# TensorE in written order in two MLPs, and block 2's norm work spread over more weight tiles

## The chip, the cores and the metric

The kernel runs on one core of one Trainium2 chip. The metric is device time of one execution in microseconds, the median of several runs. The engines are named as in the profile: PE is TensorE (PEld its weight loads), DVE is VectorE, ACT is ScalarE, POOL is GpSimd, SP is the engine whose queue issues the DMAs.

## The reference, cut to what matters

Two transformer blocks on 512 tokens of width 1024, in fp32. The change touches the MLP at the end of each.

```python
# block 1: D_FF = 4096
x = x + jnp.square(jax.nn.relu(rmsnorm(x, norm_ffn) @ ffn_w1)) @ ffn_w2
...
# block 2: D_FF_2 = 2816
u = rmsnorm_2(x, norm_ffn_w[l])
up, gate = jnp.split(u @ w_ffn_up[l], 2, axis=-1)
a = causal_dwconv_2(up, ffn_conv_w[l], ffn_conv_b[l])     # 3 taps along the tokens
x = x + (jax.nn.silu(a) * gate) @ w_ffn_down[l]
return rmsnorm_2(x, norm_final_w)
```

## The kernel before

**Tiling.** Activations are held transposed, features on the 128 partitions and 512 tokens along the row, so x is eight tiles of 128 x 512. A weight *tile* is 128 x 128; a *column* is the eight tiles that make one output tile of 128 x 512. Weights come in units of eight tiles (`wts`, 512 KB) through four `raw` buffers. Each unit, and each activation, is split into a high part (ScalarE, `S.copy` to fp32r) and a low part (VectorE, `V.tensor_sub`), five buffers `whi` and `wlo`; `mm3` (L466 to L468) multiplies with three matmuls, high x high, high x low, low x high. A plain column is 24 matmuls of 512 columns into one of four "mm" PSUM banks.

**Pairs.** Most hidden columns of both MLPs go two at a time through `pairg` (L351): seven products of 12 matmuls of 256 columns each, 84 in all, where the two plain columns would take 48 of 512, the length of 96. The products are, in order, B11, V1, B21, V7, B22, V6, T4. On the weight side they need sums of weights, each split in six steps (`seven_steps`; `sraw` the sums, `a`, `s75`, `s64`, `b` the operands). On the activation side they need differences made by `rights` (L397), three steps for each of four pairs of x tiles: s0 two ScalarE scalings, s1 five short VectorE operations (L416 to L421), s2 two splits (L534, L535). A pair fills four banks; the first is freed early by a copy `c0` (L385, ScalarE), the others by four VectorE additions (L391 to L394) into `q`. In block 1 pairs take "mm" and "sm" banks in turn; in block 2 all take the four "sm" banks. There the hidden numbers 3, 4, 6, 7, 9, 10, 12, 13, 15, 16, 18, 19 (each an up and a gate column) are pairs, the others plain.

**What is written where.** The program is emitted as straight code. `defer(n, fn)` emits `fn` once `n` more weight tiles have been taken; `wst["i"]` counts them. Tile 0 of an MLP is its first weight tile. SP's queue follows the written order (`manual_schedule` around the whole build). The order on all other engines is planned when the program is compiled: instructions are taken by a model of the machine, an earlier written one first among those that the model holds for ready, so an engine may run ahead of the written order where the model sees it wait.

**Block 1's MLP** (L1312 on): two plain and two paired hidden steps, then four groups; each takes eight down columns (`ffn_w2`) over the eight hidden tiles of its group, with the next group's pairs between them. In the last group nothing stands between its last pair (hidden 15) and its eight down columns. `rb2`, made of the sums of squares (`wide_later`, two matmuls with a matrix of ones, L621 and L622), is used when down columns are added to x; it is emitted at tile 44 (`WIDE1`).

**Block 2's MLP** (L1674 on): the input sums `acc` are split and summed by L621 and L622, the rstd row `rb` follows by a chain of VectorE operations (L628, L551 to L566, one more emitted per tile). A plain hidden (`hidden2`) is an up and a gate column, `zp` = up x `rb` (L1713), which frees the up bank, the convolution (L1590 on ScalarE, two L1592 on VectorE), silu (L1715), a product with the gate bank (L1716), a split. In a pair the same is done from `q` (`hidden7`, L1686 to L1698). Three groups, 0 to 7, 8 to 15, 16 to 21; behind each the eight down columns, with the first hidden of the next group ahead of them. The last group's down columns are done for one half of the tokens and then the other; each half ends with the sums for the final norm, one ones-matmul over seven tiles (L1794) and one over the last (L1796), fp32.

**Queues around the change.** `rb` starts at tile 3, `rights` at 5 + `VD` x pair (`VD` = 4), so at tiles 5 to 19. `zp` of hidden 0 is emitted after its two columns, at tile 16, of hidden 1 at 32, of hidden 2 at 48, where the first pair (hidden 3) begins.

Of the kernel before, what the change touches and what calls it, by code (L numbers as in the profile page):

```python
# [52 lines left out]
VD = 4  # L53
# [111 lines left out]
def build(tc, A, out, stage=99):  # L165
    nc = tc.nc
    ctx = ExitStack()
    with ctx:

        ctx.enter_context(tc.manual_schedule(engines={mybir.EngineType.SP}))  # L170
        _build(ctx, tc, nc, A, out, stage)


def _build(ctx, tc, nc, A, out, stage):
# [8 lines left out]
    def nm(s):  # L183
        cnt[0] += 1
        return f"{s}_{cnt[0]}"
# [7 lines left out]
    def tmp(shape=(P, T)):  # L193
        return ap_.tile(list(shape), F32, tag="t2", bufs=NSLOT, name=nm("tmp"))
# [4 lines left out]
    def tinyc(n):  # L199
        return ap_.tile([P, n], F32, tag=nm("tinyc"), bufs=1, name=nm("tinyc"))  # L200

    def bank(kind="mm"):
        return pp.tile([P, T], F32, tag=kind, bufs=4, name=nm(kind))
# [234 lines left out]
    def defer(n, fn):  # L438

        late.append((wst["i"] + n, fn))  # L440
        late.sort(key=lambda e: e[0])
# [84 lines left out]
    def split(src, g=None, shape=(P, T)):  # L526

        hi, lo = t2(F32R, shape), t2(F32R, shape)
        split_to(hi, lo, src, g)
        return hi, lo  # L530
# [16 lines left out]
    def rsqrt_g(r, a, lat=0.3):  # L547

        t, h = (tiny(a.shape[-1]), tiny(a.shape[-1])) if a.shape[-1] < 64 else (tmp(a.shape), tmp(a.shape))
        al = 0.375 ** 0.5  # L550
        V.tensor_scalar(r.bitcast(I32), a.bitcast(I32), -0.5, float(0x5F3759DF),  # L551
                        op0=ALU.mult, op1=ALU.add)
        yield 0.0, lat
        V.tensor_mul(t, r, r)
        yield 0.0, lat
        V.scalar_tensor_tensor(out=h, in0=t, scalar=al, in1=a, op0=ALU.mult, op1=ALU.mult)
        yield 0.0, lat
        V.scalar_tensor_tensor(out=t, in0=h, scalar=-1.25 / al, in1=h, op0=ALU.add, op1=ALU.mult)
        yield 0.0, lat
        V.scalar_tensor_tensor(out=r, in0=t, scalar=1.875, in1=r, op0=ALU.add, op1=ALU.mult)  # L560
        yield 0.0, lat
        V.tensor_mul(t, r, r)
        yield 0.0, lat
        V.scalar_tensor_tensor(out=t, in0=t, scalar=-0.5, in1=a, op0=ALU.mult, op1=ALU.mult)
        yield 0.0, lat
        V.scalar_tensor_tensor(out=r, in0=t, scalar=1.5, in1=r, op0=ALU.add, op1=ALU.mult)  # L566
# [22 lines left out]
    def row_bc(c, nt, dst=None):  # L589

        ps = bank("sm")
        for i in range(nt):
            PE.matmul(ps[:, i * P:(i + 1) * P], lhsT=c[:, i:i + 1].to_broadcast([P, P]),
                      rhs=ident, start=True, stop=True)
        r = dst if dst is not None else ap_.tile([P, T], F32, tag="t2", bufs=NSLOT, name=nm("rbc"))
        S.copy(r[:, :nt * P], ps[:, :nt * P])
        return r
# [18 lines left out]
    def wide_later(acc, eps, rbt, at, square):  # L616

        def part():
            hi, lo = split(acc)
            ps = bank("sm")  # L620
            PE.matmul(ps, lhsT=ones_r, rhs=hi, start=True, stop=False)  # L621
            PE.matmul(ps, lhsT=ones_r, rhs=lo, start=False, stop=True)  # L622
            if square:
                V.tensor_scalar(rbt, ps, 1.0 / D, eps, op0=ALU.mult, op1=ALU.add)
                V.reciprocal(rbt, rbt)
                return
            a = tmp()
            V.tensor_scalar(a, ps, 1.0 / D, eps, op0=ALU.mult, op1=ALU.add)  # L628
            step(rsqrt_g(rbt, a))

        def step(g):
            if next(g, None) is not None:
                defer(1, lambda: step(g))

        defer(at, part)

    def acc_tile():
        return ap_.tile([P, T], F32, tag="t2", bufs=NSLOT, name=nm("acc"))
# [7 lines left out]
    acc = acc_tile()  # L646
# [11 lines left out]
    rb = row_bc(rc, 4)  # L658
# [553 lines left out]
    acc = acc_tile()  # L1212
# [87 lines left out]
    acc = acc_tile()  # L1300
# [8 lines left out]
    xs = xs2  # L1309


    rb2 = acc_tile()  # L1312
    wide_later(acc, 1e-6, rb2, WIDE1, True)
    rops, steps = rights(x, "norm_ffn", xs)
# [68 lines left out]
    acc = acc_tile()  # L1383
# [4 lines left out]
    for what, n, g in ffn_order():  # L1388
# [15 lines left out]
        if n == 7:  # L1404
            for k in range(8 * g, 8 * g + 8):
                hs.pop(k)
    xs = xs2

    rc12, rc, rb, rb1 = tinyc(8), tinyc(4), acc_tile(), acc_tile()

# [251 lines left out]
    acc = acc_tile()  # L1662
# [8 lines left out]
    xs = xs2  # L1671


    rb = acc_tile()  # L1674
    wide_later(acc, 1e-5, rb, 3, False)

    rops2, steps = rights(x, "norm_ffn_w_2", xs)
    for j, f in enumerate(steps):
        defer(5 + VD * (j // 3) + j % 3, f)

    def hidden7(i):
        hl = (t2(F32R), t2(F32R))
# [77 lines left out]
    for hf in range(2):  # L1760
        ts = slice(hf * H, (hf + 1) * H)
        acc = acc_tile()
# [143 lines left out]
```

## Time and profile before

| what | value |
|---|---|
| median of 3 runs | 1552.65 us (1549.92 to 1555.24) |
| the profiled execution's own time | 1555.27 us |
| its span in the trace | 1553.5 us |
| block 1's MLP in it | about 413 to 765 us |
| block 2's MLP in it | about 1161 us to the end |
| TensorE busy | 97% of the span |
| VectorE busy | 70% of the span |

The trace is of one execution, so terms worked out from it belong to 1555.27 us. TensorE's matmuls are pipelined: the bars of neighbours overlap, and the step from one start to the next is what a matmul costs in a run of them. The granted clock of a stretch (PEclk) is a share of TensorE's full speed.

### The profile page before, as it was taken

How to read it: one execution, taken by the hardware profiler on the slowest of the kernel's cores; microseconds unless marked ns; L12 is line 12 of the kernel's file. 1: busy time of each engine (PE TensorE's matmuls, PEld its weight loads, DVE VectorE, ACT ScalarE, POOL GpSimd, SP SyncE). 2: the span in 40 equal slices, each digit the busy share in tenths (PEclk: the TensorE clock that was granted, in tenths of full speed). 3: DMA queues.
4: the chain of work that ended last, by engine and by line, in shares of the span. 5: the costliest groups of instructions: out<-in, count | busy, mean ns of one | idle time of the engine just before them, and what ended most of it. 6: DMA issues, size and time to landing. Idle time of an engine off the chain costs nothing.

```text
span 1553.5 us, 21399 instructions
## 1 busy us (share of the span) xinstructions
PE 1512.2 (97%) x8336; PEld 1292.5 (83%) x8336; DVE 1080.4 (70%) x1759; ACT 705.8 (45%) x1169; POOL 147.9 (10%) x162
## 2 busy tenths in 40 slices
PE   8999999999999999999999999999998899999996
PEld 6887898888888888888888888888887888988886
DVE  6887685554786787766688677245547877887667
ACT  6665555443564353535354344333334442443343
POOL 0002110200201211011400000000020002002101
PEclk9999999999999999999999999999999999999999
DMA  6033335221222233223043222222221232224221
GB/s 252 22 108 99 114 133 190 96 68 55 82 91 87 95 108 103 95 97 122 23 161 122 82 75 81 83 93 91 97 93 43 93 122 80 84 82 136 77 74 55
DMA packets 51509, 149.94 MB, mean 97 GB/s; under 512 B 9552, under 2 KB 14032, under 8 KB 51408
## 3 DMA queue, kind: packets, MB, share of 16 engines
q1 hardware_dynamic: 51264, 148.32, 28.5%
q8 instruction: 65, 1.06, 0.3%
q14 instruction: 36, 0.29, 0.1%
q10 hardware_dynamic: 144, 0.26, 0.1%
HBM read 143.97 MB, written 3.28 MB: 95 GB/s over the span
## 4 chain that ended last, share of the span: by engine, by line
PE 88%; DVE 6%; ACT 3%; issue 1%; DMA 1%; SPq 0%; POOL 0%; DVEq 0%; ACTq 0%; POOLq 0%
PE mm L466 23%; PE mm L468 23%; PE mm L467 23%; PE sm L468 4%; PE sm L466 4%; PE sm L467 4%; DMA raw<-wts 1%; ACT whi L263 1%; DVE wlo L315 1%; DVE wlo L265 1%; ACT whi L310 1%; ACT t L1095 0%; DVE wlo L267 0%; PE sm L586 0%; DVE t L1807 0%
## 5 line engine op out<-in xcount | busy, mean ns | idle before, releaser
L466 PE MATMUL mm<-t,whi 128*128 128x512 f32 (+1 forms) x1696 | 646.6, 381 | 10.3 <-ACT whi L259 6.7
L468 PE MATMUL mm<-t,wlo 128*128 128x512 f32 (+1 forms) x1696 | 643.2, 380 | 1.9 <-DVE wlo L267 1.4
L467 PE MATMUL mm<-t,whi 128*128 128x512 f32 (+1 forms) x1696 | 642.9, 379 | 0.2 <-DVE t L535 0.2
L466 PEld LDWEIGHTS mm<-t,whi 128*128 128x128 f32 x1696 | 320.2, 189 | 71.2 <-ACT whi L259 6.7
L468 PEld LDWEIGHTS mm<-t,wlo 128*128 128x128 f32 x1696 | 320.2, 189 | 67.3 <-DVE wlo L267 2.7
L467 PEld LDWEIGHTS mm<-t,whi 128*128 128x128 f32 x1696 | 320.3, 189 | 61.5 <-DVE t L538 0.5
L263 ACT CAST whi<-raw 128x1024 fp32r<-128x1024 f32 x202 | 211.3, 1051 | 303.3 <-PE mm L467 138.6
L265 DVE TENSOR_TENSOR wlo<-raw,whi 128x1024 fp32r<-128x1024 f32 x189 | 236.5, 1252 | 78.1 <-ACT whi L263 77.7
L466 PE MATMUL sm<-t,whi 128*128 128x256 f32 (+1 forms) x464 | 132.0, 285 | 4.2 <-ACT t L534 2.3
L467 PE MATMUL sm<-t,whi 128*128 128x256 f32 (+1 forms) x464 | 131.7, 284 | 0.5 <-DVE t L535 0.5
L468 PE MATMUL sm<-t,wlo 128*128 128x256 f32 (+1 forms) x464 | 131.7, 284 | 0.0
L580 POOL TENSOR_TENSOR acc<-acc,tmp 128x512 f32<-128x512 f32 (+1 forms) x37 | 52.8, 1432 | 467.7 <-ACT tmp L576 463.9
L315 DVE TENSOR_TENSOR wlo<-sraw,whi 128x1024 fp32r<-128x1024 f32 x52 | 72.9, 1404 | 34.6 <-ACT whi L310 34.2
L310 ACT CAST whi<-sraw 128x1024 fp32r<-128x1024 f32 x52 | 54.5, 1048 | 88.0 <-PE mm L467 69.3
L466 PEld LDWEIGHTS sm<-t,whi 128*128 128x128 f32 x464 | 88.1, 190 | 5.9 <-ACT t L534 2.5
L467 PEld LDWEIGHTS sm<-t,whi 128*128 128x128 f32 x464 | 88.2, 190 | 1.6 <-DVE t L535 0.7
L468 PEld LDWEIGHTS sm<-t,wlo 128*128 128x128 f32 x464 | 88.2, 190 | 0.4
L1441 DVE TENSOR_TENSOR tmp<-mm,acc 128x512 f32<-128x512 f32 x46 | 31.7, 689 | 48.9 <-PE mm L468 46.9
L1398 POOL TENSOR_TENSOR res<-res,tmp 128x512 f32<-128x512 f32 x24 | 38.9, 1636 | 250.0 <-DVE tmp L1396 236.0
L310 ACT CAST whi<-raw 128x1024 fp32r<-128x1024 f32 x26 | 27.3, 1050 | 67.7 <-PE mm L467 37.0
L466 PE MATMUL sm<-t,t 128*128 128x256 f32 (+1 forms) x156 | 47.0, 302 | 7.3 <-ACT t L310 7.0
L302 DVE TENSOR_TENSOR sraw<-raw,raw 128x1024 f32<-128x1024 f32 x26 | 33.0, 1269 | 25.3 <-DMA raw<-wts 25.2
(384 smaller groups left out, 1971.9 us busy)
## 6 DMA issues: line engine op xcount, KB each, us to landing
raw<-wts SPq DMA_DIRECT2D x259, 512.0 KB, 3.3
res<-xT SPq DMA_DIRECT2D x16, 256.0 KB, 5.5
yT<-t SPq DMA_DIRECT2D x6, 256.0 KB, 2.2
tmp<-tmp SPq DMA_DIRECT2D x20, 64.0 KB, 2.0
gm<-gm SPq DMA_DIRECT2D x4, 256.0 KB, 4.5
dn<-ch SPq DMA_DIRECT2D x4, 256.0 KB, 2.3
tmp<-memT SPq DMA_DIRECT2D x4, 256.0 KB, 2.7
cst<-const SPq DMA_DIRECT2D x1, 576.0 KB, 6.9
```

The costliest lines, as they stand in the source:

```text
L263: S.copy(hi, r)
L265: defer(LO, lambda r=r, hi=hi, lo=lo: V.tensor_sub(lo, r, hi.bitcast(F32)))
L302: V.tensor_tensor(t["s75"].rearrange("p (a b) -> p a b", a=2), r3, r1[:, T:].unsqueeze(1).to_broadcast([P, 2, T]), op=ALU.add)
L310: S.copy(t[n][0], s)
L315: V.tensor_sub(t[n][1], src(), t[n][0].bitcast(F32))
L466: PE.matmul(ps, lhsT=ahi, rhs=bhi, start=start, stop=False)
L467: PE.matmul(ps, lhsT=ahi, rhs=blo, start=False, stop=False)
L468: PE.matmul(ps, lhsT=alo, rhs=bhi, start=False, stop=stop)
L580: eng.tensor_add(acc[:, :w], acc[:, :w], dst[:, :w])
L1398: G.tensor_add(x[n], x[n], t)
L1441: V.tensor_mul(t, ps, rb)
```

## The change

All TensorE instructions of block 1's MLP, and all from block 2's MLP to the end of the kernel, are put in a region in which TensorE issues in the written order. The other engines' order, and which of their instructions stands beside which, is planned as before, around that. In block 2's MLP the input sums and the rstd row start at tile 8 in place of 3, and the three steps of each pair of `rights` at 10, 18, 26 and 34 in place of 5, 9, 13 and 17.

```diff
+    mlp = ExitStack()
+    mlp.enter_context(tc.manual_schedule(engines={mybir.EngineType.PE}))
     rb2 = acc_tile()
     wide_later(acc, 1e-6, rb2, WIDE1, True)
     rops, steps = rights(x, "norm_ffn", xs)
...
             for k in range(8 * g, 8 * g + 8):
                 hs.pop(k)
     xs = xs2
+    mlp.close()
...
+    ctx.enter_context(tc.manual_schedule(engines={mybir.EngineType.PE}))
     rb = acc_tile()
-    wide_later(acc, 1e-5, rb, 3, False)
+    wide_later(acc, 1e-5, rb, 8, False)
 
     rops2, steps = rights(x, "norm_ffn_w_2", xs)
     for j, f in enumerate(steps):
-        defer(5 + VD * (j // 3) + j % 3, f)
+        defer(10 + 8 * (j // 3) + j % 3, f)
```

## Rows read from the trace of the kernel before

**Rows 1.** Page, part 1: busy us, share of the span, instructions of an engine

```profile
PE 1512.2 (97%) x8336; PEld 1292.5 (83%) x8336; DVE 1080.4 (70%) x1759; ACT 705.8 (45%) x1169; POOL 147.9 (10%) x162
```

**Rows 2.** By stretch: length, busy PE, PEld, DVE, ACT, POOL (instructions), PEclk, DMA, GB/s

```profile
468.30:474.50 6.20, 4.37 (x15) 3.40 (x14) 6.17 (x9) 2.46 (x5) 0.00 (x0) 0.72 0.38 137
...
726.00:764.80 38.80, 38.80 (x169) 31.38 (x168) 25.89 (x33) 21.39 (x31) 19.49 (x21) 1.00 0.13 41
1161.40:1184.00 22.60, 22.60 (x99) 18.31 (x98) 21.15 (x34) 10.75 (x15) 0.20 (x2) 1.00 0.20 70
1184.00:1198.20 14.20, 9.55 (x38) 7.55 (x37) 9.53 (x16) 6.98 (x10) 0.20 (x2) 0.76 0.00 0
...
1207.50:1218.60 11.10, 6.29 (x30) 5.99 (x30) 8.02 (x12) 5.16 (x9) 0.10 (x1) 0.69 0.14 48
1218.60:1265.00 46.40, 45.94 (x333) 42.95 (x332) 39.85 (x53) 22.15 (x30) 0.30 (x3) 1.00 0.33 107
...
1386.00:1393.00 7.00, 4.51 (x25) 4.00 (x24) 5.23 (x7) 3.27 (x6) 0.10 (x1) 0.76 0.22 75
...
1161.40:1265.00 103.60, 93.68 (x541) 82.61 (x540) 84.08 (x123) 50.15 (x68) 0.81 (x8) 0.93 0.22 73
...
1467.00:1482.00 15.00, 15.00 (x129) 15.00 (x129) 9.83 (x12) 6.60 (x8) 0.00 (x0) 1.00 0.37 116
```

**Rows 3.** Timeline, TensorE, head of block 2's MLP; [idle before <-releaser]

```profile
1188.70 0.39 PE L466 MATMUL sm<-t,whi 128*128 128x256 f32 x1 [2.34 <-ACT t L534]
...
1191.90 0.80 PE L466 MATMUL mm<-t,whi 128*128 128x512 f32 x1 [1.81 <-DVE zp L1713]
...
1212.64 0.58 PE L466 MATMUL sm<-t,t 128*128 128x256 f32 x1 [4.81 <-ACT t L310]
```

**Rows 4.** Timeline, VectorE, the same head

```profile
1166.89 0.69 DVE L535 TENSOR_TENSOR t<-acc,t 128x512 fp32r<-128x512 f32 x1
...
1177.10 0.68 DVE L566 SCALAR_TENSOR_TENSOR acc<-tmp,acc 128x512 f32<-128x512 f32 x1
...
1186.43 0.42 DVE L416 TENSOR_TENSOR t<-t,t 128x256 f32<-128x256 f32 x1
...
1191.16 0.68 DVE L1713 TENSOR_TENSOR zp<-mm,acc 128x512 f32<-128x512 f32 x1
```

**Rows 5.** Timeline, three engines, end of block 1's MLP

```profile
716.52 0.39 PE L466 MATMUL mm<-t,whi 128*128 128x512 f32 x1
...
722.61 1.14 ACT L1363 CAST t<-q 128x512 fp32r<-128x512 f32 x2
...
723.26 1.29 DVE L1368 TENSOR_TENSOR t<-q,t 128x512 fp32r<-128x512 f32 x2 [2.96 <-ACT t L1363]
```

**Rows 6.** Timeline, TensorE, between the two token halves at the end

```profile
1521.81 0.28 PE L466 MATMUL mm<-t,whi 128*128 128x256 f32 x1
...
1524.19 0.70 PE L1794 MATMUL sm<-acc,cst 128*128 128x256 f32 x2
...
1525.09 0.65 PE L1796 MATMUL sm<-acc,cst 128*128 128x256 f32 x2
```

**Rows 7.** Timeline, three engines, from hidden 6 to hidden 7

```profile
1252.24 0.40 PE L466 MATMUL mm<-t,whi 128*128 128x512 f32 x1
...
1253.32 0.50 PE L468 MATMUL mm<-t,wlo 128*128 128x512 f32 x1 [0.46 <-DVE wlo L267]
...
1253.37 0.36 ACT L385 COPY t<-sm 128x256 f32<-128x256 f32 x1
...
1255.52 0.69 DVE L391 TENSOR_TENSOR q<-sm,t 128x512 f32<-128x512 f32 x1
```

**Rows 8.** Timeline, TensorE, first pair of block 1's MLP

```profile
442.08 0.38 PE L466 MATMUL mm<-t,t 128*128 128x256 f32 x1 [1.54 <-ACT t L310]
...
443.47 0.33 PE L468 MATMUL mm<-t,t 128*128 128x256 f32 x1
```

**Rows 9.** Timeline, TensorE, first down column of block 1's MLP

```profile
470.55 0.38 PE L466 MATMUL sm<-t,whi 128*128 128x256 f32 x1 [1.83 <-ACT whi L310]
```

## The prediction, made before the change was run

> **What bounds the kernel now.** I read the share of busy time first: TensorE is busy 97% of the span [rows 1]. So only two things can move the time: places where TensorE waits, and places where its granted clock is low. The second view cuts the span into stretches and counts matmuls in each [rows 2]. Its two undisturbed rows give the price of one step. In 726.0 to 764.8 us 168 steps of 512 columns take 38.8 us, 0.231 us each; in 1467 to 1482 some 127 steps of 256 columns (129 with those that its edges cut) take 15.0 us, 0.118 us each. With these two numbers any stretch can be priced, and what is over is lost.
>
> In 1184.0 to 1198.2 there are 38 matmuls, 21 of 256 and 17 of 512 columns: 2.5 + 3.9 = 6.4 us of work in 14.2, 7.8 us lost. In 1207.5 to 1218.6 there are 30 of 256 columns, 3.5 us of work in 11.1: 7.6 lost. Both are at the head of block 2's MLP, together 15.4 us. In 468.3 to 474.5, near the head of block 1's MLP, 4 short and 9 long steps (2.6 us) leave 3.6 lost, and in 1386 to 1393 25 short steps leave 4.1 lost [rows 2]. The granted clock in these four rows is 0.69 to 0.76, so each loss is a wait and then some steps at the lower of the two clock levels, 1.2 GHz instead of 2.4.
>
> The timeline of the head of block 2's MLP says why. TensorE had taken 21 matmuls of the first paired columns (hidden 3) ahead of the last plain ones (hidden 2), and waited 2.34 us for a split of `rights`; then 1.81 us for the first `zp` (L1713), which frees the PSUM bank that up column 2 wants; then 4.81 us for the fourth weight operand of the pair [rows 3]. On VectorE the rstd row `rb` ends at 1177.8 (L566), but L1713 starts only at 1191.16, with the five subtractions and splits of three pairs of `rights` in front of it (the third at 1186.43) [rows 4]. `rights` was emitted at tiles 5 to 19, `zp` of hidden 0 at tile 16.
>
> **The change, part by part.** No instruction is added or removed; orders change. The moved steps issue work on ScalarE, VectorE and (two matmuls) TensorE, no DMA and nothing on POOL, and SP's order stays as written.
>
> *Spread of rb and rights (block 2).* The sums start at tile 8 instead of 3, `rights` at 10, 18, 26, 34 instead of 5, 9, 13, 17. Now only the first pair of `rights` is written ahead of `zp` of hidden 0, so `zp` can follow `rb` at about 1177.8. Up column 2 wants its bank when the four columns before it are done, at about 1184 where the first pair's matmuls begin [rows 2], and hidden 3, after two more columns of 5.55 us, starts near 1195; the last `rights`, written at tile 36, has until then. Both waits of [rows 3] would be covered. The floor is VectorE: it did 84.1 us of work in the 103.6 us from 1161.4 to 1265.0. At the 86% that it reached in 1218.6 to 1265.0 that takes 97.8 us, a gain of 5.8; at the 94% of 1161.4 to 1184.0 it takes 89.4, a gain of 14.2 [rows 2]; all of the loss is 15.4. I take 92%, near the upper row because there, as here, its queue was never empty: 91.4 us, a gain of 12.2. The two ones-matmuls on the input sums now stand at tile 8, one column of 5.55 us behind the stage's begin at 1161.4, so at 1167.0. The low half of the sums is there at 1167.58 [rows 4]: TensorE waits up to 0.6; I count 0.4.
>
> *Written order, end of block 1's MLP.* The last group of eight down columns comes right behind its last pair, whose 84 matmuls end at 716.5. The squares of that pair are split on ScalarE from 722.61 (two of 0.57) and on VectorE from 723.26 to 724.55 [rows 5]. TensorE now fills this with tiles of later columns. In written order it does six tiles of the first (18 x 0.231 = 4.2 us, to 720.7), waits for the seventh and is through with the eighth at 725.1. By then it has done 24 matmuls; before, in the same 8.6 us without a gap, 37. Cost 13 x 0.231 = 3.0 us; queued behind are the other seven columns, and block 2 behind these. Behind a wait of 1.83 us [rows 9] the clock was low and cost 1.8 more (3.6 lost less 1.83). Bounds 3.0 to 4.8; I take 3.9.
>
> *Written order, end of block 2's MLP.* Each half of the tokens ends with the sums for the final norm, L1794 and L1796. TensorE now runs 24 matmuls of the second half before and between them, from 1521.81 on; the sums start at 1524.19 and the last ends near 1525.7 [rows 6]. In written order those 24 come behind: 24 x 0.118 = 2.8 us, and up to 1.8 of low clock. Bounds 2.8 to 4.6; I take 3.7. Queued behind L1794 are then all columns of the second half, and the tail waits for them.
>
> *Written order, pair behind pair.* The second pair of a plain-pair-pair cycle needs a "sm" bank that the copy `c0` (L385) frees. At 1252.2 the copy is late (1253.37 on ScalarE), and the next bank comes with L391 at 1255.52 on VectorE; TensorE fills with nine 512-column matmuls and loses 0.46 us of wait, 0.7 in all [rows 7]. In written order it waits to 1253.8 and again from 1255.3 to 1256.2: 2.6 instead of 0.7, 1.9 worse. The pattern stands three times (1253, 1361, 1397): 5.7. Below, it can be nothing, as the place of the copy in ScalarE's queue is planned anew. I take half, 2.9. For this repeating gap the Trainium skill (Perfetto Trace Analysis, section Optimization Strategy of Identifying Performance Opportunities) says that the same gap repeating on the engine that should be saturated can mean too little SBUF or PSUM for the next tile. The rows agree so far that a bank copy stands beside each gap; by that rule a new order would not help and the whole 5.7 would be paid, 2.8 us more than my sum.
>
> *Written order, third product of a pair.* Four times, first at 442.08, the low half of operand `b` is later than the high half, and matmuls of the fourth product fill in (TensorE takes it up at 443.47 [rows 8]). In written order that wait shows: 1.0 us there, 0.4 to 0.5 at 461, 1246 and 1353, 2.4 in all; nothing if `b` is planned earlier. I take 2.0.
>
> *The two other losses* (468, 1386) wait for ScalarE's queue (L310), which the change does not touch by itself. They could vanish (7.7 with the clock) or grow by what TensorE no longer fills (some 3). I count a gain of 1.5.
>
> **The sum.** Gain 12.2 + 1.5 = 13.7; cost 0.4 + 3.9 + 3.7 + 2.9 + 2.0 = 12.9. Net 0.8 us shorter. The profiled execution took 1555.27 us (a span of 1553.5), 2.6 above the median of 1552.65, so I put the new median at 1551.9: the head of block 2's MLP is won, and the places that TensorE had filled out of order give it back. Three runs of before lie 5.3 us apart; about 0.3%, 4.7 us, is what a measurement can tell from no change.
>
> The Trainium skill (Perfetto Trace Analysis, Matmul Optimizations) warns that TensorE's power follows its use, so that matmuls should run back to back. The trace shows it: clock 0.72 around a wait of 1.83 us [rows 2, 9]. It speaks against the two end pieces; at full price for both the sum would be 1.8 us longer.
>
> **Rivals.** *The new waits get covered (faster).* VectorE's and ScalarE's orders are planned around TensorE's; with a fixed TensorE, copies and splits may come on time. Then only the data waits of the two ends stay (3.0 + 2.8 + 0.4 = 6.2), against 14.4 of the 15.4 and 3.5 of the 7.7: 11.7 shorter, 1541. For it: at the head VectorE's order, not its work, is the cause [rows 4]. Against: at the two ends the chain of data itself is late [rows 5, 6].
>
> *VectorE stays the floor (slower).* Behind the head come pairs 3, 4, 6, 7, where VectorE is 86% busy. If it does no better than that, the gain is 5.8, and every new wait is paid in full: 4.8 + 4.6 + 5.7 + 2.4 + 0.4 = 17.9. That is 12.1 longer, 1564.8. It decides once the head's gain falls under the written order's price; at full price that is for any gain up to 15.4, at mine below 12.9 less the 1.5. For it: the 86%. Against: that stretch also did weight splits for later columns.
>
> *The change does little of what it says.* Where nothing waits, as in 726 to 764.8, TensorE already follows the written order; and the plan for VectorE might keep `zp` behind `rights`. Then 1552.65.
>
> **How the numbers follow.** Chances: forecast 0.44 (1545 to 1559), covered waits 0.28 (1541), VectorE's floor 0.22 (1564.8), little 0.06. The forecast's own range is its bounds: gain 5.8 to 15.4, ends 5.8 to 9.4, pairs 0 to 5.7. Of it 0.08 lies under 1548.0, 0.07 above 1557.3. Faster: 0.28 + 0.08 = 0.36; same 0.29 + 0.06 = 0.35; slower 0.22 + 0.07 = 0.29. The range goes from 1538, a little below the covered waits, to 1565, the floor itself, and leaves out some 0.2.
>
> **What the profile of after would show.** Right: `zp` of hidden 0 within 2 us behind L566; no matmul of 256 columns before the sixth plain column; the stretch from up column 0 to the end of hidden 7 some 12 us shorter; a TensorE wait of about 2.5 us in the first of block 1's last eight down columns, and one of about 2.3 at the first L1794, neither there before. Wrong: `zp` still behind the second and third `rights`; no wait at those two ends; or waits of 2 us and more inside hidden 3 to 7 in place of the old ones, which would be VectorE's floor.

## The result and the profile after

| | us, median (lowest to highest) | against the kernel before (95% interval) |
|---|---|---|
| before | 1551.66 (1549.92 to 1555.24) | 1 |
| after | 1570.32 (1566.77 to 1570.69) | 1.0112 (1.0088 to 1.0136) |
| predicted | 1551.9 (1538 to 1565) | |

The change makes the kernel 1.1% slower. The time lies above the range, and above the 1564.8 of the rival "VectorE stays the floor". The profiled execution of after took 1570.69 us with a span of 1568.9, 15.4 more than the span of before. (The profiled execution of before was one of its longer ones, so the medians lie 18.7 apart, the spans 15.4.)

Page of after, the head and part 1, columns as in [rows 1]:

```profile
span 1568.9 us, 21401 instructions
...
PE 1515.6 (97%) x8336; PEld 1294.9 (83%) x8336; DVE 1081.1 (69%) x1759; ACT 706.0 (45%) x1169; POOL 147.3 (9%) x162
```

The instruction counts are those of before [rows 1], and the busy times lie within 3.4 us of them: nothing was added. The share of busy time shows nothing of a change of order. The 3.4 us more on TensorE go with a slightly lower granted clock, 0.989 over the span where before had 0.991. So the 15 us are waits, and steps at the lower clock behind them.

Stretches of after, columns as in [rows 2]: the first pair of block 1, the end of its MLP, the head of block 2's MLP, hidden 6, two places where a pair stands behind a pair, the pair whose matmuls lost 4.1 us near 1386 in before (they now run some 10 us later), and the sums between the token halves:

```profile
436.50:446.00 9.50, 6.78 (x40) 6.16 (x39) 7.32 (x11) 6.22 (x13) 0.00 (x0) 0.82 0.33 109
721.00:729.00 8.00, 5.37 (x17) 3.72 (x16) 3.02 (x6) 4.39 (x6) 0.00 (x0) 0.79 0.28 87
1203.00:1220.20 17.20, 8.07 (x38) 7.01 (x37) 12.02 (x20) 7.06 (x12) 0.20 (x2) 0.60 0.09 30
1247.50:1254.50 7.00, 5.52 (x31) 5.10 (x31) 4.16 (x7) 1.86 (x3) 0.10 (x1) 0.76 0.23 77
1258.00:1264.00 6.00, 3.73 (x29) 3.35 (x29) 5.34 (x8) 2.78 (x5) 0.00 (x0) 1.00 0.43 124
1369.00:1376.50 7.50, 4.69 (x36) 4.14 (x35) 7.13 (x10) 2.56 (x5) 0.00 (x0) 1.00 0.59 192
1394.00:1401.00 7.00, 6.25 (x52) 6.00 (x51) 5.17 (x7) 3.40 (x6) 0.10 (x1) 1.00 0.21 75
1529.00:1541.00 12.00, 9.75 (x63) 8.97 (x62) 8.48 (x22) 4.38 (x11) 0.00 (x0) 0.86 0.01 2
...
1167.10:1212.50 45.40, 36.99 (x168) 29.82 (x166) 38.07 (x61) 22.78 (x32) 0.31 (x3) 0.93 0.13 47
```

They are read with the step prices of the prediction. In 1203.0 to 1220.2, 38 short steps are 4.5 us of work, so 12.7 of 17.2 are lost. In 1394 to 1401, 52 short steps are 6.1 of 7.0 us, so of the old loss near 1386 about 1 us is left. The last row is for VectorE: from the first up column of block 2's MLP to the end of the long wait it was busy 38.07 of 45.4 us, 84%.

Timeline of after, TensorE, the rows with the waits (idle time and its releaser in brackets):

```profile
440.23 0.39 PE L466 MATMUL mm<-t,t 128*128 128x256 f32 x1 [1.81 <-ACT t L310]
441.47 0.57 PE L468 MATMUL mm<-t,t 128*128 128x256 f32 x1 [0.73 <-DVE t L315]
...
724.37 0.50 PE L466 MATMUL mm<-t,whi 128*128 128x512 f32 x1 [2.41 <-ACT t L1366]
...
1213.12 0.58 PE L466 MATMUL sm<-t,whi 128*128 128x256 f32 x1 [8.22 <-ACT t L534]
...
1260.32 0.39 PE L466 MATMUL sm<-t,whi 128*128 128x256 f32 x1 [1.38 <-ACT t L385]
1262.88 0.35 PE L466 MATMUL sm<-t,whi 128*128 128x256 f32 x1 [0.89 <-DVE q L391]
...
1398.12 0.39 PE L468 MATMUL sm<-t,t 128*128 128x256 f32 x1 [0.75 <-DVE t L315]
...
1535.34 0.70 PE L1799 MATMUL sm<-acc,cst 128*128 128x256 f32 x2 [2.11 <-DVE acc L580]
```

Where [rows 3] had three long waits at the head, there is one of 8.22 us, for the last pair of `rights`. Most other rows are places where before showed no such wait, since TensorE took something else meanwhile [rows 5 to 7]; at the first pair of block 1 one of 1.54 us has become 1.81 and 0.73 [rows 8], and at 1398 a short wait for the low half of `b` is what is left of the old one.

The same head on VectorE and ScalarE, timeline of after:

```profile
1183.85 0.69 DVE L566 SCALAR_TENSOR_TENSOR acc<-tmp,acc 128x512 f32<-128x512 f32 x1
1184.58 0.69 DVE L1718 TENSOR_TENSOR zp<-mm,acc 128x512 f32<-128x512 f32 x1
...
1202.52 1.23 DVE L315 TENSOR_TENSOR wlo<-sraw,whi 128x1024 fp32r<-128x1024 f32 x1
1203.66 1.29 DVE L535 TENSOR_TENSOR t<-t,t 128x512 fp32r<-128x512 f32 x2
1204.86 0.68 DVE L1718 TENSOR_TENSOR zp<-mm,acc 128x512 f32<-128x512 f32 x1
...
1205.64 0.72 ACT L1594 ACTIVATE tmp<-zp,colt 128x512 f32<-128x512 f32 x1 [2.12 <-DVE zp L1718]
1207.97 0.72 ACT L1720 ACTIVATE tmp<-tmp,colt 128x512 f32<-128x512 f32 x1 [1.61 <-DVE tmp L1596]
1209.45 0.62 ACT L534 CAST t<-tmp 128x512 fp32r<-128x512 f32 x1 [0.75 <-DVE tmp L1721]
1209.97 0.72 ACT L410 ACTIVATE t<-res,colt 128x512 f32<-128x512 f32 x1
```

The first `zp` follows `rb` at once, as wanted (in [rows 4] it started 13 us behind the end of it). But the `zp` of hidden 1 comes only at 1204.86, behind a weight split and the splits of `rights`, and the scalings for the last `rights` (L410) stand in ScalarE's queue behind that hidden's chain, at 1209.97.

To account for the whole, I take for each matmul the time to the start of the next one, less its step price, and add up what is over (us):

| place | before | after | change | predicted |
|---|---|---|---|---|
| head of block 2's MLP, to hidden 4 | 16.0 | 13.5 | -2.6 | -12.2 and +0.4 |
| operand `b` of hidden 6 (1248) | 0 | 3.6 | +3.6 | in the row of third products |
| end of block 1's MLP (721) | 0 | 4.6 | +4.6 | +3.9 |
| sums between token halves (1530) | 0.7 | 5.0 | +4.2 | +3.7 |
| pair behind pair (1259, 1369, 1405) | 2.2 | 9.1 | +6.9 | +2.9 |
| third products (438, 463, 1361) | 2.6 | 6.8 | +4.2 | +2.0 |
| the two others (468, and 1386, in after 1397) | 8.0 | 3.4 | -4.6 | -1.5 |
| sum | | | +16.3 | -0.8 |

Over the whole trace it is +15.5; of the -0.8 left over, 0.5 lies ahead of block 1's MLP, the rest is spread over small differences. The short fp32 steps of the sums between the halves are priced like the others, so 0.7 to 0.8 us of that row stands there without any wait.

### The profile page after: what moved, and what is told of

It reads as the page before. It is cut to its first block, busy times and chain, and to the rows that moved or that the text cites. A ratio compares the mean times of both kernels' runs of the same rounds, so it can differ in the third digit from the quotient of the medians.

```text
span 1568.9 us, 21401 instructions
## 1 busy us (share of the span) xinstructions
PE 1515.6 (97%) x8336; PEld 1294.9 (83%) x8336; DVE 1081.1 (69%) x1759; ACT 706.0 (45%) x1169; POOL 147.3 (9%) x162
## 4 chain that ended last, share of the span: by engine, by line
PE 85%; DVE 8%; ACT 4%; issue 2%; DMA 1%; SPq 0%; POOL 0%; DVEq 0%; ACTq 0%; POOLq 0%
PE mm L466 23%; PE mm L468 23%; PE mm L467 23%; PE sm L468 4%; PE sm L466 4%; PE sm L467 4%; DVE wlo L265 1%; ACT whi L263 1%; DVE wlo L315 1%; DMA raw<-wts 1%; ACT whi L310 1%; DVE t L535 1%; DVE t L315 0%; DVE q L391 0%; DVE tmp L1596 0%
## 5 line engine op out<-in xcount | busy, mean ns | idle before, releaser
L310 ACT CAST whi<-sraw 128x1024 fp32r<-128x1024 f32 x52 | 54.6, 1050 | 93.9 <-PE mm L467 65.2
L310 ACT CAST whi<-raw 128x1024 fp32r<-128x1024 f32 x26 | 27.3, 1052 | 59.3 <-PE mm L467 32.8
L302 DVE TENSOR_TENSOR sraw<-raw,raw 128x1024 f32<-128x1024 f32 x26 | 32.7, 1259 | 26.3 <-DMA raw<-wts 26.2
```

What stands on the lines that cost most here:

```text
L302: V.tensor_tensor(t["s75"].rearrange("p (a b) -> p a b", a=2), r3, r1[:, T:].unsqueeze(1).to_broadcast([P, 2, T]), op=ALU.add)
L310: S.copy(t[n][0], s)
```

## Experiments

Two theories on the written order: A, each matmul that the planner took out of order covered a wait that now shows; against it, that the order costs by what it does to other queues. On the head of block 2's MLP: F, VectorE's work up to the first pair is the floor; O, the planned order of VectorE's and ScalarE's queues makes the wait; B, the spread itself costs. "The head lost" below means the sum of the first two rows of the table: 16.0 before, 17.0 after.

### One part alone

Written order in block 1's MLP only (of the change, only this is kept):

```diff
+    mlp = ExitStack()
+    mlp.enter_context(tc.manual_schedule(engines={mybir.EngineType.PE}))
...
+    mlp.close()
```

> The kernel before with TensorE in written order in block 1's MLP alone. Theory A (each matmul that the planner had taken out of order covered a wait, and the wait now shows): the waits at 438 to 445 and at 721 to 728 of the trace of the changed kernel come back, block 1's MLP is 6 to 7 us longer, block 2 is as before; 1558 us. Rival B (the written order itself costs little, the loss is made where the norm work was spread in block 2): within 2 us of the kernel before.

Measured 1561.22 us, ratio 1.0064 (1.0049 to 1.0079). Its places lost what they lose in after: 5.1 at 438, 0.7 at 463, 4.7 at 722; block 2's head stayed at 15.2. The median rose by more than the 7 us that theory A expected; the trace itself is 5.7 us longer than the one of before.

Written order from block 2's MLP on, with the tiles of before:

```diff
+    ctx.enter_context(tc.manual_schedule(engines={mybir.EngineType.PE}))
     rb = acc_tile()
     wide_later(acc, 1e-5, rb, 3, False)
```

> The kernel before with TensorE in written order from block 2's MLP on, the norm work at its old tiles. Theory A: the ones-matmuls at tile 3 wait some 4 us for the input sums, up column 2 waits some 7 us for the late eviction of up column 0, then no matmul of hidden 3 waits as long as 4.8 us; pair behind pair, third products and the sums between the token halves cost 8 to 10 us as in the changed kernel; 1558 to 1566 us, so the spread was worth some 2 to 5 us of it. Rival B: the spread is what costs, so this is within 3 us of the kernel before.

Measured 1559.69 us, ratio 1.0051 (1.0036 to 1.0066); the trace is of the shortest execution, 1556.83. The pairs lost 2.8, 3.6 and 2.8 us, the third products 1.0 each, as in after. The head lost 13.2, in other places: 5.4 at the ones-matmuls, which at tile 3 come before the sums are there (TensorE's timeline), and 5.8 at operand `b`. The wait of some 7 us that was expected at up column 2 did not come.

```profile
1163.49 0.49 PE L621 MATMUL sm<-t,ones_r 128*128 128x512 f32 x1 [2.67 <-ACT t L534]
...
1204.84 0.38 PE L466 MATMUL sm<-t,t 128*128 128x256 f32 x1 [3.60 <-ACT t L310]
```

The spread alone, TensorE planned freely:

```diff
-    wide_later(acc, 1e-5, rb, 3, False)
+    wide_later(acc, 1e-5, rb, 8, False)
-        defer(5 + VD * (j // 3) + j % 3, f)
+        defer(10 + 8 * (j // 3) + j % 3, f)
```

> The kernel before with the new tiles for the input sums and rights, TensorE planned freely. Theory A: the first eviction follows the rstd row at once, but the last rights still come behind hidden 1's convolution, so the head of block 2's MLP loses 12 to 15 us instead of 15.4; 1548 to 1552 us. Rival B (the spread is what costs): 4 us or more above the kernel before.

Measured 1554.06 us, ratio 1.0015 (1.0006 to 1.0025). This is 3.2 us above before, between the two expectations. The head lost 17.4, with the very wait of after, freely planned as TensorE was:

```profile
1206.63 0.58 PE L466 MATMUL sm<-t,whi 128*128 128x256 f32 x1 [8.22 <-ACT t L534]
```

So that wait belongs to the spread, and it comes whether TensorE's order is planned or written. The two written orders alone, 0.64% and 0.51%, add up to about after's 1.12%; the spread took nothing off.

After with the `rights` written closer together:

```diff
-        defer(10 + 8 * (j // 3) + j % 3, f)
+        defer(10 + 4 * (j // 3) + j % 3, f)
```

> The changed kernel with rights at tiles 10, 14, 18 and 22 in place of 10, 18, 26 and 34, so the last pair of rights is written ahead of the first eviction of hidden 1 (tile 32). Theory O (the 8.2 us wait of hidden 3 is an order: the last rights stood behind hidden 1's chain on ScalarE): that wait falls under 3 us and the time by 5 to 8 us, 1562 to 1566 us. Theory F (VectorE is the floor there, whatever its order): the wait comes back at another place of hidden 1 to 4 and the time stays within 2 us of the changed kernel, 1568 to 1572.

Measured 1565.70 us, ratio 1.0092 (1.0077 to 1.0107). The wait for the `rights` went, as O has it, with a time in O's range; one for the pair's fourth weight operand took its place, as F has it. The head lost 13.2:

```profile
1213.16 0.58 PE L466 MATMUL sm<-t,t 128*128 128x256 f32 x1 [6.84 <-ACT t L310]
```

### The two ends, filled by hand

After, with other work written into the two end waits; the order of the weights in HBM (`weight_order`) is changed to match, and the norm of the first token half becomes the function `tail0`:

```diff
-        ps = lin("ffn_w2", n, range(8 * g, 8 * g + 8), hs)
...
+        elif n == 0:
+            last = [lin("ffn_w2", m, range(24, 30), hs, stop=False) for m in range(2)]
+            for m in range(2):
+                lin("ffn_w2", m, (30, 31), hs, ps=last[m], start=False)
...
             part(n, range(nk - 1, nk) if hf == 0 and n < 3 else range(nk))
+            if hf == 1 and n == 0:
+                tail0()
```

> The changed kernel with two places filled by hand, TensorE still in the written order. (1) In the last group of block 1's MLP the first six tiles of down columns 0 and 1 are written one behind the other, and only then the last two tiles of each. (2) In the final part the two ones-matmuls and the whole norm of the first token half are written behind the first column of the second half. Theory A (each matmul that the planner took out of order covered a wait that the written order shows): the loss at the end of block 1's MLP falls from 4.6 us to under 1, for 18 more 512-column steps (4.2 us) stand ahead of the late squares; the loss between the token halves falls from 5.0 us to under 1.5, for 24 steps (2.8 us) stand ahead of a wait of 2.1; some 7 to 8 us in all, so about 1563 where the changed kernel took 1570. Rival (the written order costs by itself, as by other queues that are planned around it): the two waits come back at the next tile or column, and the time stays at 1568 to 1571.

Measured 1563.30 us, ratio 1.0073 (1.0052 to 1.0093), against 1.0112. The two stretches by the table of engines:

```profile
716.00:728.00 12.00, 11.87 (x57) 9.51 (x56) 7.79 (x11) 6.04 (x8) 0.00 (x0) 1.00 0.53 175
1519.00:1531.00 12.00, 11.86 (x95) 11.12 (x94) 8.37 (x20) 6.97 (x16) 0.00 (x0) 1.00 0.00 1
```

TensorE is busy 99% in both; the loss fell from 4.6 to none and from 5.0 to 1.2. This is theory A at these two places: the wait is the cost, and independent work longer than the wait, written into it, covered it.

### The head: order or work

VectorE and ScalarE in the written order too, to the end of hidden 3:

```diff
+    hd = ExitStack()
+    hd.enter_context(tc.manual_schedule(engines={mybir.EngineType.DVE, mybir.EngineType.Activation}))
     rb = acc_tile()
...
+        if i == 4:
+            hd.close()
```

> The changed kernel with VectorE and ScalarE in the written order too, from the sums ahead of block 2's MLP to the end of hidden 3. In the changed kernel's trace VectorE did 5.1 us of work on pair 4's weights (1.22, 0.69, 0.69, 1.23, 1.23) ahead of the rights that hidden 3 was waiting for; these are written later and now come later. Theory O (the 8.2 us wait in hidden 3 is a matter of VectorE's and ScalarE's planned order): the wait falls by about 5 to some 3 us, the clock does not fall as long, the stage is 5 to 8 us shorter, and the time is about 1564. Theory F (VectorE's work is the floor): what hidden 3 gains, hidden 4 pays when it has to wait for its own weights; the loss over hidden 3 and 4 together stays at 14 to 18 us and the time at 1568 to 1571.

Measured 1576.16 us, ratio 1.0157 (1.0133 to 1.0180). The 8.22 us wait is gone, and the head lost 22.8 instead of 17.0: 5.29 and 1.43 us for plain weights, whose ScalarE copies now stand behind a hidden's chain, which itself waits 4.75 us for `zp`, and 2.98 behind the first pair's sums. Neither theory expected it to get worse. So the planner's order of the two queues was better than the one order tried against it; that no order does better isn't shown by it. ScalarE and TensorE:

```profile
1185.12 0.72 ACT L1594 ACTIVATE tmp<-zp,colt 128x512 f32<-128x512 f32 x1 [4.75 <-DVE zp L1722]
...
1189.44 1.04 ACT L263 CAST whi<-raw 128x1024 fp32r<-128x1024 f32 x1
...
1190.53 0.79 PE L466 MATMUL mm<-t,whi 128*128 128x512 f32 x1 [5.29 <-ACT whi L263]
1206.20 0.50 PE L466 MATMUL mm<-t,whi 128*128 128x512 f32 x1 [1.43 <-ACT whi L263]
...
1230.11 0.39 PE L466 MATMUL sm<-t,whi 128*128 128x256 f32 x1 [2.98 <-DVE q L391]
```

After with less work on VectorE; this kernel leaves out the low halves of three pairs of `rights`:

```diff
-                vs = split(st["v"])
-                ws = split(st["w"])
+                if p < few:
+                    vs, ws = (t2(F32R), xs[2 * p][1]), (t2(F32R), xs[2 * p + 1][1])
+                    S.copy(vs[0], st["v"])
+                    S.copy(ws[0], st["w"])
...
-    rops2, steps = rights(x, "norm_ffn_w_2", xs)
+    rops2, steps = rights(x, "norm_ffn_w_2", xs, 3)
```

> The changed kernel with six instructions fewer on VectorE at the head of block 2's MLP, and nothing else: the low halves of the first three pairs of rights are not split off (six of 0.68 us, 4.1 us), and their matmuls read low halves of the plain operand in their place; this leaves out part of the computation. ScalarE's and TensorE's work and all orders as written stay. Theory F (VectorE's work up to hidden 3 is the floor): the 8.2 us wait in hidden 3 falls by about 4, the loss there from 13.0 to 8 or 9, and the time from 1570 to about 1565. Rival S (ScalarE's queue is the cause: the last scalings stand behind hidden 1's chain, whose steps wait for each other and for their bank): the wait stays within 1 us of 8.2, and the time at 1568 to 1571.

Measured 1561.51 us, ratio 1.0068 (1.0048 to 1.0087). The wait fell by 4.2 us for 4.1 us of VectorE work, at the same place (the edit moves L534 to L539):

```profile
1208.44 0.58 PE L471 MATMUL sm<-t,whi 128*128 128x256 f32 x1 [4.01 <-ACT t L539]
...
1202.50:1214.00 11.50, 7.19 (x40) 6.33 (x39) 8.80 (x15) 5.77 (x10) 0.10 (x1) 0.70 0.15 46
```

The head lost 9.8, 7.2 less: the wait itself, less time at the lower clock behind it, and 1.6 less at hidden 6. It is as theory F says, and against the rival that ScalarE's queue alone sets the wait. It does not refute O: taking steps out of a queue also lets what stands behind them start earlier. Nor is it a pure test of work, for the planner also put one weight split (1.23 us) behind the `zp` of hidden 1 that stands ahead of it in after. And in the 8.22 us wait of after VectorE itself stood idle for 2.9 us (0.85, 0.79, 0.69 and 0.54), while steps of hidden 1 and of `rights` went to ScalarE and back.

Before with the first pair one hidden later:

```diff
-SEVEN2 = {3, 4, 6, 7, 9, 10, 12, 13, 15, 16, 18, 19}
+SEVEN2 = {4, 6, 7, 9, 10, 12, 13, 15, 16, 18, 19}
```

> The kernel before with one size changed: hidden 3 of block 2 is computed as two plain columns, so that the first pair is hidden 4. TensorE has 48 steps of 0.231 us in place of 84 of 0.118: 1.2 us more. VectorE has some 8 us less to do before hidden 7 and 11 us more time until the first pair. Theory F (VectorE's work up to the first pair is what makes the two waits at the head): of the 15 us lost there at most 7 are left, and the time is 1540 to 1546. Theory O (the order of zp behind rights on VectorE makes the first wait, whatever time there is): up column 2 and 3 wait for their bank as before, 7 us or more are lost there still and the rest of the 15 is won, 1545 to 1549. If the waits only move to the second pair: 1552 to 1554.

Measured 1543.85 us, ratio 0.9947 (0.9928 to 0.9966): faster than both kernels. The head lost 3.4 instead of 16.0, for 1.2 us more of matmuls:

```profile
1150.00:1250.00 100.00, 96.96 (x528) 82.47 (x528) 80.60 (x118) 49.49 (x68) 4.60 (x11) 1.00 0.24 85
```

TensorE is busy 97% where it was 90% in the 103.6 us of [rows 2], and VectorE 81%, as before: it has the same rate, but the first pair starts later, and VectorE has one pair's weight sums less to make. The two are not told apart here.

### With room on VectorE, does order matter?

The hand-filled kernel (written order, spread) with `SEVEN2` of the last one:

```diff
-SEVEN2 = {3, 4, 6, 7, 9, 10, 12, 13, 15, 16, 18, 19}
+SEVEN2 = {4, 6, 7, 9, 10, 12, 13, 15, 16, 18, 19}
```

> The hand-filled kernel of the second experiment call (e6: written order, both ends filled, spread as in the change), with hidden 3 of block 2 computed as two plain columns. Theory F: the loss of 13 us at the head falls to 4 or less, for 1.2 us more of TensorE work, so about 1563 less 8 to 10, 1553 to 1555; written order then costs, against the kernel before with the same size (1543.9), what its places show that were not filled: 2.8 at MLP1's first pair, three waits of a pair behind a pair (some 2.0 to 2.8 each) and some 1.0 each at third products, 9 to 11 us in all. Rival (written order stalls at the head whatever VectorE has to do): 8 us and more are still lost there, 1558 or more.

Measured 1562.02 us, ratio 1.0069 (1.0049 to 1.0089). Here F failed: the head still lost 12.9. TensorE and then VectorE, timelines (helper lines are 3 higher, L313 is L310):

```profile
1201.12 0.77 PE L469 MATMUL mm<-t,whi 128*128 128x512 f32 x1 [4.11 <-DVE zp L1728]
...
1192.35 1.23 DVE L318 TENSOR_TENSOR wlo<-sraw,whi 128x1024 fp32r<-128x1024 f32 x1 [2.30 <-ACT whi L313]
...
1200.29 0.68 DVE L1728 TENSOR_TENSOR zp<-mm,acc 128x512 f32<-128x512 f32 x1
```

The first column of hidden 3 waits for its bank until the `zp` of hidden 1 is done, and that stands on VectorE behind two pairs of `rights` and behind a weight split that waited 2.30 us for its high half. This is a matter of order, and in written order TensorE has nothing else to take. Written order with before's tiles at this size was not run, so it stays open how much of the 12.9 is the written order and how much the spread.

The same with the `rights` closer together:

```diff
-        defer(10 + 8 * (j // 3) + j % 3, f)
+        defer(10 + 4 * (j // 3) + j % 3, f)
```

> The kernel of e10 (written order, both ends filled, hidden 3 as two plain columns) with the rights written at tiles 10, 14, 18, 22 in place of 10, 18, 26, 34; the sums stay at tile 8. In e10 the head still lost 6.8 and 4.1 us: zp of hidden 1 started 4.1 us after up column 4 wanted its bank, behind two pairs of rights and a split that waited 2.3 us for its high half. Theory B (the spread itself makes this wait, by putting rights behind hidden 0's chain and ahead of hidden 1's on VectorE): with the rights through earlier the 4.1 us wait falls under 1.5, the head loses 4 to 6 in all, and the time is 1555 to 1558. Rival (VectorE's work is too much for written order wherever the rights stand): the wait moves, to hidden 0's zp or to the pair's operand b, 9 us or more are lost and the time is 1560 to 1563.

Measured 1559.47 us (1556.21 to 1560.32), ratio 1.0042 (1.0027 to 1.0057). Between the two: the wait for `zp` grew to 6.14, the losses at operand `b` of the first pair (4.1) and of hidden 6 (2.0) vanished, and the head lost 7.8. Theory B named the wrong wait, but the closer `rights` cost less.

Before with three pairs less (`NPLAIN` is the number of plain hidden columns ahead of block 1's first pair):

```diff
-NPLAIN = 2
+NPLAIN = 3
-SEVEN2 = {3, 4, 6, 7, 9, 10, 12, 13, 15, 16, 18, 19}
+SEVEN2 = {4, 6, 7, 9, 10, 12, 13, 16, 18, 19}
```

> The kernel before with three pairs computed as plain columns: hidden 3 and hidden 15 of block 2 and hidden 2 of block 1's MLP. Each costs TensorE 1.2 us and takes work from VectorE ahead of a place where a pair's last weight operand was late: against the kernel with hidden 3 alone so changed (1543.9), the 4.7 us lost near 1374 and the 4.4 us lost over 437 to 470 are at stake. Theory F: 3 of each come back for 1.2 each, so 1539 to 1541. Rival (these two waits are latencies of the weights' chain, not work): they move to the next pair, and the time is 1545 to 1547.

Measured 1534.97 us, ratio 0.9895 (0.9876 to 0.9915), the fastest kernel here. The 4.4 us lost over 437 to 470 and the 4.7 near 1374 are gone wholly, more than F expected; of the rest, 1.6 near 1317 went too.

The same with the spread:

```diff
-    wide_later(acc, 1e-5, rb, 3, False)
+    wide_later(acc, 1e-5, rb, 8, False)
-        defer(5 + VD * (j // 3) + j % 3, f)
+        defer(10 + 8 * (j // 3) + j % 3, f)
```

> The kernel of e11 (three pairs computed as plain columns, TensorE planned freely) with the spread of the change: sums at tile 8, rights at 10, 18, 26, 34. Theory B (the spread puts rights ahead of hidden 1's zp): the head of block 2's MLP loses 3 to 6 us more than the 4.2 of e11, and the time is 1538 to 1541. Rival (where VectorE has time enough the tiles do not matter): the head loses 3 to 5 as in e11, and the time is 1534 to 1536.

Measured 1542.14 us, ratio 0.9926 (0.9908 to 0.9944): by the medians 7 us slower than without the spread. The head lost 11.3 instead of 4.2, but not at hidden 1's `zp`. TensorE and ScalarE:

```profile
1235.22 0.58 PE L466 MATMUL sm<-t,t 128*128 128x256 f32 x1 [6.42 <-ACT t L310]
...
1228.77 1.04 ACT L310 CAST whi<-sraw 128x1024 fp32r<-128x1024 f32 x1 [3.31 <-PE sm L467]
1229.72 0.72 ACT L1590 ACTIVATE tmp<-zp,colt 128x512 f32<-128x512 f32 x1
1232.55 0.72 ACT L1694 ACTIVATE tmp<-tmp,colt 128x512 f32<-128x512 f32 x1 [2.12 <-DVE tmp L1592]
1234.03 0.62 ACT L1697 CAST t<-tmp 128x512 fp32r<-128x512 f32 x1 [0.76 <-DVE tmp L1695]
1234.56 0.61 ACT L310 CAST t<-raw 128x512 fp32r<-128x512 f32 x1
```

The short copy of operand `b` (0.61 us) stands in ScalarE's queue behind a copy that waited 3.31 us for TensorE and behind a hidden's chain of waits. So the spread has a price of its own once VectorE has room: here a weight copy of the next pair came later. Why the planner puts `b` there was not tried.

## Why the prediction was wrong

**The step that failed is the size of the head's gain.** The cause of the old waits was read rightly from [rows 3] and [rows 4], and the cure did what it should: `zp` at 1184.58 right behind `rb`, and no plain column waits for its bank. But I let VectorE work at 92% over the stage and took 12.2 us. It was busy 84% up to the end of the long wait and 84.70 us in the 104.4 from 1167.1 to 1271.5, 81% as before. The row I leaned on, 94% in 1161.4 to 1184.0 [rows 2], is of a stretch where work stood ready for it; later in the stage its weight splits wait for copies of ScalarE (0.57, 0.39 and 0.94 us), and two of the copies for buffers that TensorE frees (3.22 and 1.03 us). Even the lower end, 86%, was too high. The two head rows of the table came to +1.0 us, not -11.8. A share of busy time over a stage was also the wrong measure: what counts is the work that must be done before the first pair. The last `rights`, written from tile 34 on, came 8 us after 1204.9, when hidden 3 wanted them. Their place in the code was part of the change, and the prediction took them to be in time.

**The costs of written order were seen at the right places and taken too low.** At the end of block 1's MLP 4.6 (bounds 3.0 to 4.8, taken 3.9), between the halves 4.2 (2.8 to 4.6, taken 3.7), at the ones-matmuls 0.5 (0.4): the mechanism as described, the waits 2.41 and 2.11 near the 2.5 and 2.3 foretold; both went when they were filled by hand. For a pair behind a pair I took half of 5.7 because the copy's place "is planned anew"; the waits stayed near the size that I had read, and 6.9 was paid, over the upper bound: 1.38 and about 0.89 us stand three times, at 1369 with 0.54 more. By the Trainium skill (Perfetto Trace Analysis, Identifying Performance Opportunities), the same gap repeating on the engine that should be saturated can mean that SBUF or PSUM is short for the next tile. The price that I drew from it, the whole 5.7, was nearer to the 6.9; whether more banks would have closed the gaps was not tried. For the third products my bound of 2.4 was too low: three places cost 4.2, and the fourth, hidden 6, another 3.6. I had counted the wait for the low half of `b` alone; in written order at the first pair the high half was later too, 1.81 us against the 1.54 of [rows 8], with 0.73 for the low half behind it. Hidden 6 is no cost of the written order alone: with the spread and a free TensorE it waited as well (2.3 us lost in one step at 1245).

**The two other losses** gave back 4.6 instead of 1.5: near 1386 the wait for the high half of `b` went and 1.0 for the low half stayed, and at [rows 9] 2.1 us of wait stayed without the low clock.

**The sum.** The terms as measured are -2.6 + 3.6 + 4.6 + 4.2 + 6.9 + 4.2 - 4.6 = +16.3. With the head's two rows as I put them, the time would have been some 13 us lower, about 1557, inside my forecast's own range of 1545 to 1559. The other terms of the written order were some 7 us over what I took, without hidden 6, and the other losses gave 3 back.

**The rivals.** "VectorE stays the floor", with chance 0.22, came nearest in its mechanism, though the runs do not part work from order, and in its time was still 5 us short: it too gave the head a gain (5.8), where there was a loss of 1.0, and its price list of 17.9 stood against some 20. Its sign, waits of 2 us and more inside hidden 3 to 7 in place of the old ones, is the 8.22 us row. "The new waits get covered" fell: of the new waits none was covered. The Trainium skill (Perfetto Trace Analysis, Matmul Optimizations) warns that TensorE's power is scaled by its use, so matmuls should run back to back. At the two ends the trace agrees, with a granted clock of 0.79 and 0.86; full price at both was 9.4, and 8.8 was measured.

**What stays open:** with VectorE's full work six orders of the head lost 13.2 to 22.8 us; that no order does better isn't shown, nor is the effect of more buffers for ScalarE's weight copies. With less work, order decided between 3.4 and 12.9.

## What to carry to other kernels

Before fixing an engine's order by hand, list each place where it now runs something early and find what it would wait for there: such waits came back here, at the two ends with 4.6 and 4.2 us, and went when independent work was written into them. When a consumer waits on a loaded engine, count the work that must be done before the date, not a busy share over the stage; moving steps later in the code relieved one wait here and delayed the next. If that work comes too late in every order that you try, give the engine less work or a later date: here three pairs computed plainly cost 3.5 us of matmuls, and the kernel was 16 us faster.

## What the runs showed of the hardware

A wait of about 2 us did not always bring the clock down. Around the first down column of block 1's MLP the granted clock was 0.72 in before (wait 1.83 us [rows 9]) and 1.00 in after (wait 2.12):

```profile
470.00:476.00 6.00, 3.88 (x22) 3.20 (x21) 5.96 (x8) 3.19 (x5) 0.00 (x0) 1.00 0.53 176
```

Between the token halves, a wait of 2.11 us in after went with 0.86 over 12 us and 4.2 us lost above before, and one of 2.10 in the kernel with less VectorE work with 1.00 and 3.5 lost above before:

```profile
1523.00:1531.00 8.00, 5.75 (x42) 4.95 (x41) 5.97 (x16) 3.56 (x9) 0.00 (x0) 1.00 0.00 0
```

So a wait of about 2 us cost from 2.4 to 4.2 us. Two waits of 1.38 and 0.89 us, 2.6 us apart, left the clock at 1.00 (1258 to 1264 and 1369 to 1376.5 above). The 8.22 us wait went with 0.60.
